# Seven block products instead of eight in the mLSTM's x and z projections of a one-core block kernel

## Chip, core and metric

One core of a Trainium2 chip runs the whole kernel. The metric is the device time of one execution in microseconds (us): the median of 3 runs is 1810.85 us, from 1810.42 to 1810.91.

## What is computed

The input is one sequence of 512 tokens with 1024 channels in f32. It goes through a first block (a gated feed-forward net, FFN; a mixer of two attentions; a second FFN) and a second block (an mLSTM mixer, then an RG-LRU mixer, with a final norm). The change touches the mLSTM:

```python
proj = u @ w_in                       # u: 512 x 1024, normed
xm, z, o_pre, i_pre, f_pre = split(proj)          # xm, z, o_pre: 512 x 2048
xc = silu(causal_dwconv(xm, conv_w, conv_b))      # 4 taps
q, k = per head: xc @ w_q, xc @ w_k               # 4 heads, 512 -> 256
v = per head: xm @ w_v                            # 512 -> 512
h_tilde = mlstm_chunkwise(q, k, v, log_i, log_f)
hh = sigmoid(o_pre) * h_tilde                     # then a norm over each head: hn
y = (hn * norm_w + skip * xc) * silu(z)
x = x + y @ w_out
```

## The kernel before, in words

Channels lie on the 128 partitions, tokens on the 512 columns. Every weight product is made of three matmuls (`mm3`, L112): each operand is split into a rounded part `hi` (fp32r) and the remainder `lo`, and hi\*hi, hi\*lo and lo\*hi add up in PSUM. A weight tile of 128 x 1024 is loaded by SyncE's queue into one of 4 `raw` tiles; ScalarE copies it to `hi` (L98), VectorE subtracts to get `lo` (L100); there are 5 tiles of each (`wload`, L93). A *group* (L148) is 24 matmuls of 512 columns: one block of 128 output channels over 8 blocks of input channels.

**The pairs of the FFN.** Both FFNs already use a seven-product scheme (Winograd's form of Strassen's) for most gate and up blocks: `Pair` (L223) and `pair_products` (L301). Two groups, 2 x 24 matmuls of 512 columns, become 7 products of 12 matmuls of 256 columns. A pair needs three split weight tiles and a half one: the top blocks (`a11`, `a12`), differences (`s1`, `s3`) from `r2`, for which GpSimd's queue issues a DMA that adds a weight from memory onto a tile (L212), two sums on VectorE (L247, L248) with their split (`s2`, `s4`), and `a22` (L251). The activations need eight combinations, made once by `xhalves` (L264), which fill 12 tiles of the pool `act` (40) and 16 of the 18 of the pool `chain`. VectorE joins the products from PSUM (L323 to L325, L335). A pair's weights are made during the pair before (`nxt`); the first pair of a run has no pair before it.

**The mLSTM** (L706 to L985) makes x, z and the output gate o by plain groups. `x_proj(hd)` and `z_proj(hd)` are four groups each, `o_proj(hd)` (L854) 96 matmuls of 512 columns. Its order is the list at L958 to L985: for heads 0 to 2 `scores`, `o_proj` (`v_proj` for head 0), `numer`, `z_proj` of the next head, `y_out`, `x_proj`, `v_proj` and `x_conv` of the next head, `out_proj`, `qk_proj`; head 3 closes. `residual` (L784) stands before `qk_proj(0)`.

**What sets the order.** Every engine has one queue and works it in order. The order in each queue is planned when the kernel is built: instructions are ranked by their place in the program, moved forward by the offset of `high_priority` (75 for weights, 100 for reads out of PSUM), and of those whose inputs and buffers the planner expects to be ready the first is taken. So matmuls of a later part may be put between those of an earlier one. DMAs of SyncE, ScalarE and GpSimd wait in that engine's queue until their buffer is free and their source is there.

Of the kernel before, what the change touches and what calls it, by code (L numbers as in the profile page):

```python
# [8 lines left out]
F32 = mybir.dt.float32  # L9
# [5 lines left out]
P = 128  # L15
# [22 lines left out]
NVEC = _n  # L38
PAD = 478


@with_exitstack
def kernel(ctx: ExitStack, tc: tile.TileContext, a, out):
# [11 lines left out]
    xp = ctx.enter_context(tc.tile_pool(name="xp", bufs=18))  # L55
    vp = ctx.enter_context(tc.tile_pool(name="vp", bufs=5))
    pp = ctx.enter_context(tc.tile_pool(name="pp", bufs=4, space=PSUM))
    qp = ctx.enter_context(tc.tile_pool(name="qp", bufs=4, space=PSUM))
# [164 lines left out]
    class Pair:  # L223


        def __init__(self, top, low):
            self.top, self.low, self.w = top, low, {}

# [22 lines left out]
        def last(self):  # L251
            with tc.high_priority(offset=BOOST):
                t = vp.tile([P, T + 32], F32, tag="v", name="v")
                nc.sync.dma_start(t[:, :T], self.low[:, T:])
                hi = vp.tile([P, T + 32], F32R, tag="v", name="v")
                S.copy(hi[:, :T], t[:, :T])
                lo = vp.tile([P, T + 32], F32R, tag="v", name="v")
                V.tensor_tensor(lo[:, :T], t[:, :T], f(hi[:, :T]), op=ALU.subtract)
            self.w["a22"] = cut((hi, lo), slice(0, T))
# [43 lines left out]
    def pair_products(pair, b, nxt, between):  # L303
# [30 lines left out]
        with tc.high_priority(offset=EVAC):  # L334
            V.tensor_tensor(t[:, HT : 3 * HT], c3, v, op=ALU.add)  # L335
        g, u = t[:, :T], t[:, T:]
        S.activation(g, g, AF.Silu)
# [3 lines left out]
    def ffn(x, gain, gu, dn, pre=None):  # L341
# [50 lines left out]
        for j in range(4, KF):  # L392
            nxt = Pair(gu[2 * j + 2], gu[2 * j + 3]) if j + 1 < KF else None
            job = down_job(j)
            job(-1)
            new.append(pair_products(cur, b, nxt, job))
            cur = nxt
            if j % 4 == 3 and j < 19:
                old, new = new, []
# [306 lines left out]
    def mlstm(x):  # L706
# [30 lines left out]
        skq = cp.tile([P, 16], F32, tag="skq", name="skq")  # L737
        V.tensor_copy(skq, vc("msk", 0, 16))
        R = slice(0, 4)
        gT, em, cT = (cp.tile([P, 16], F32, tag=n, name=n) for n in ("gT", "em", "cT"))  # L740
# [49 lines left out]

        def z_proj(hd):
            st[hd]["z2"] = [silu2(group(wload(a["mh"][hd][4 + j]), xs), rb) for j in range(4)]

        def x_proj(hd):
            xm, xr = [], []
            for j in range(4):
                ps = pre.pop(0) if pre else group(wload(a["mh"][hd][j]), xs)
                t = act_tile()
# [3 lines left out]
                xr.append(t)  # L802
            st[hd].update(xm=xm, xr=xr)

        def x_conv(hd):
            xc2, xcs = [], []
            for j, t in enumerate(st[hd].pop("xr")):
                c = conv(t, "mcw", 16, "mcb", 4 * hd + j)
# [26 lines left out]
        def qk_proj(hd):  # L835
            xcs = st[hd].pop("xcs")
            qk = []
            for i in range(2):
                w = wload(a["mh"][hd][12 + i])
                w3 = tuple(z.rearrange("p (k m) -> p k m", k=4) for z in w)  # L840
                both = gp.tile([P, 2 * T], F32R, tag="four", name="four")
                for m in range(2):
                    ps = bank()
                    for k in range(4):
                        mm3(ps, tuple(z[:, k, m * P : (m + 1) * P] for z in w3), xcs[k], k == 0, k == 3)
                    hi, lo = both[:, m * T : (m + 1) * T], act_tile(F32R)
                    scale = (1.0 / 16, 1.0)[i]
                    with tc.high_priority(offset=EVAC):
                        S.activation(hi, ps, AF.Copy, scale=scale)
                        V.scalar_tensor_tensor(lo, ps, scale, f(hi), op0=ALU.mult, op1=ALU.subtract)  # L850
                    qk.append((hi, lo))
            st[hd]["qk"] = qk

        def o_proj(hd):  # L854
# [9 lines left out]
            for b in range(4):  # L864
                t = ctile()
                with tc.high_priority(offset=EVAC):
                    S.activation(t, ops[b], AF.Tanh, scale=rsh[:, b : b + 1])
                ot.append(t)
            st[hd]["o"] = ot

        def scores(hd):
            qk = st[hd].pop("qk")
            ps = cbank()
            for b in range(4):
                c = 4 * b + hd
                PE.transpose(ps[:, b * P : (b + 1) * P], cT[:, c : c + 1].to_broadcast([P, P]), ident)
            cb = ctile()
            V.tensor_copy(cb, ps)
            sm = []
            for s in range(4):  # L880
                n = T - s * P
                ps = cbank()
                for k in range(2):
                    mm3(ps[:, :n], cut(qk[2 + k], slice(s * P, s * P + P)), cut(qk[k], slice(s * P, T)), k == 0, k == 1)
                e = ctile()
                V.tensor_scalar(e[:, :n], cb[:, s * P :], gT[:, 4 * s + hd : 4 * s + hd + 1], 0.0,
# [47 lines left out]
        def y_out(hd):  # L934
            qp, xc2, z2 = st[hd].pop("o"), st[hd].pop("xc2"), st[hd].pop("z2")
            ys = []
            for j in range(4):
# [6 lines left out]
                V.tensor_tensor(xc2[j], xc2[j], z2[j], op=ALU.mult)  # L944
                ys.append(split(xc2[j], ctile))
# [35 lines left out]
        numer(3)  # L981
# [19 lines left out]

    def conv(t, w, nt, b, i):
        c = act_tile()
        V.tensor_scalar(c, t, vc(w, 3 * nt + i), vc(b, i), op0=ALU.mult, op1=ALU.add)
        for j in range(2, -1, -1):
            s = 3 - j
            V.scalar_tensor_tensor(c[:, s:], t[:, : T - s], vc(w, j * nt + i), c[:, s:], op0=ALU.mult, op1=ALU.add)
        return c
# [297 lines left out]
```

## Time and profile before

| | |
|---|---|
| median of 3 runs | 1810.85 us |
| the profiled execution | 1810.93 us |
| its span, first to last instruction | 1809.1 us |
| TensorE (PE) busy | 1788.8 us, 99% |
| weight loads of TensorE (PEld) | 1518.8 us, 84% |
| VectorE (DVE) busy | 1244.5 us, 69% |
| ScalarE (ACT) busy | 813.7 us, 45% |
| GpSimd (POOL) busy | 66.0 us, 4% |
| mean granted clock of TensorE | 0.999 |
| DMA | 198.10 MB, mean 109 GB/s |

A matmul's row in the trace lasts longer than the distance to the next one, since matmuls overlap; their pace is read from start to start. The busy time of an engine in a stretch counts overlapping instructions once. The stretch of the mLSTM goes from 1059.5 to 1570.3 us of the span.

### The profile page before, as it was taken

Reading aid. Unit: us, or ns where it says so; the run is one execution under the profiler, and the core shown is the slowest. Engines: PE = TensorE matmul, PEld = TensorE weight load, DVE = VectorE, ACT = ScalarE, POOL = GpSimd, SP = SyncE. Lnnn points to the kernel's source line nnn. Section 1 sums busy time; section 2 is a strip of 40 time slices with the busy share of each in tenths; the row PEclk is TensorE's granted clock in tenths of the full one; section 3 lists DMA queues with packets and bytes.
Section 4 is the critical chain, followed back from the end, with each engine's and each line's share of the span. In section 5 each row is a group of like instructions: output and inputs, shape, how many; then the busy total and the mean of one; then the engine's idle time right before and its main releaser. Section 6 shows DMA issues by size and latency. Waiting matters only on the chain.

```text
span 1809.1 us, 24746 instructions
## 1 busy us (share of the span) xinstructions
PE 1788.8 (99%) x9684; PEld 1518.8 (84%) x9684; DVE 1244.5 (69%) x1992; ACT 813.7 (45%) x1207; POOL 66.0 (4%) x90
## 2 busy tenths in 40 slices
PE   8999999999999999999999999999999999999998
PEld 6899999887776688799999988888888888888887
DVE  7977777735656465887777766758366566777775
ACT  5443344524345433443444444535334444456762
POOL 1000000000000000010000000000000000000000
PEclk9999999999999999999999999999999999999999
DMA  7465555433322123265556432223222231322312
GB/s 230 113 167 155 149 153 133 140 105 97 102 82 68 50 94 105 69 171 154 153 154 155 119 108 90 71 93 94 73 92 92 67 108 59 102 91 87 99 61 73
DMA packets 74805, 198.10 MB, mean 109 GB/s; under 512 B 8000, under 2 KB 8128, under 8 KB 74688
## 3 DMA queue, kind: packets, MB, share of 16 engines
q1 hardware_dynamic: 63024, 174.35, 29.9%
q0 software_dynamic: 9792, 18.88, 6.5%
q10 hardware_dynamic: 1872, 3.29, 0.6%
q8 instruction: 76, 1.25, 0.3%
q14 instruction: 41, 0.34, 0.1%
HBM read 193.08 MB, written 2.10 MB: 108 GB/s over the span
## 4 chain that ended last, share of the span: by engine, by line
PE 92%; DVE 4%; ACT 2%; issue 1%; DMA 1%; SPq 0%; DVEq 0%; POOLq 0%; POOL 0%; ACTq 0%
PE bank L113 23%; PE bank L114 23%; PE bank L115 23%; PE cbank L113 5%; PE cbank L115 5%; PE cbank L114 5%; PE cbank L633 1%; PE cbank L601 1%; DVE chain L124 1%; PE cbank L907 1%; PE cbank L908 1%; PE cbank L909 1%; DVE act L271 1%; PE cbank L570 0%; DVE act L124 0%
## 5 line engine op out<-in xcount | busy, mean ns | idle before, releaser
L113 PE MATMUL bank<-act,hi 128*128 128x512 f32 (+1 forms) x1660 | 617.6, 373 | 8.4 <-ACT act L139 7.0
L114 PE MATMUL bank<-act,hi 128*128 128x512 f32 (+1 forms) x1660 | 615.4, 371 | 0.6 <-DVE act L140 0.5
L115 PE MATMUL bank<-act,lo 128*128 128x512 f32 (+1 forms) x1660 | 614.1, 371 | 0.7 <-DVE lo L100 0.7
L98 ACT CAST hi<-raw 128x1024 fp32r<-128x1024 f32 (+2 forms) x210 | 212.3, 1014 | 424.9 <-PE bank L114 194.8
L113 PEld LDWEIGHTS bank<-act,hi 128*128 128x128 f32 x1660 | 313.2, 189 | 66.6 <-ACT act L139 7.0
L115 PEld LDWEIGHTS bank<-act,lo 128*128 128x128 f32 x1660 | 313.5, 189 | 55.8 <-issue 1.9
L114 PEld LDWEIGHTS bank<-act,hi 128*128 128x128 f32 x1660 | 313.4, 189 | 55.3 <-DVE act L140 2.6
L100 DVE TENSOR_TENSOR lo<-raw,hi 128x1024 fp32r<-128x1024 f32 (+2 forms) x210 | 246.6, 1175 | 100.7 <-ACT hi L98 99.7
L218 ACT CAST hi<-raw 128x1024 fp32r<-128x1024 f32 x140 | 146.1, 1049 | 231.5 <-PE cbank L114 107.3
L220 DVE TENSOR_TENSOR lo<-raw,hi 128x1024 fp32r<-128x1024 f32 x140 | 170.7, 1224 | 82.4 <-ACT hi L218 78.5
L113 PE MATMUL cbank<-chain,hi 128*128 128x256 f32 x432 | 122.3, 283 | 1.7 <-ACT hi L218 1.7
L115 PE MATMUL cbank<-chain,lo 128*128 128x256 f32 x432 | 122.3, 283 | 0.9 <-DVE lo L220 0.9
L114 PE MATMUL cbank<-chain,hi 128*128 128x256 f32 x432 | 122.2, 283 | 0.0
L113 PE MATMUL cbank<-act,hi 128*128 128x256 f32 (+1 forms) x264 | 88.2, 334 | 0.0
L114 PE MATMUL cbank<-act,hi 128*128 128x256 f32 (+1 forms) x264 | 87.6, 332 | 0.0
L115 PE MATMUL cbank<-act,lo 128*128 128x256 f32 (+1 forms) x264 | 87.5, 332 | 0.0
L113 PE MATMUL bank<-hi,act 128*128 128x512 f32 x224 | 87.5, 391 | 0.0
L115 PE MATMUL bank<-hi,act 128*128 128x512 f32 x224 | 87.5, 391 | 0.0
L114 PE MATMUL bank<-lo,act 128*128 128x512 f32 x224 | 87.2, 389 | 0.0
L113 PEld LDWEIGHTS cbank<-chain,hi 128*128 128x128 f32 x432 | 82.7, 192 | 3.5 <-ACT hi L218 2.1
L115 PEld LDWEIGHTS cbank<-chain,lo 128*128 128x128 f32 x432 | 82.8, 192 | 1.4 <-DVE lo L220 1.1
L114 PEld LDWEIGHTS cbank<-chain,hi 128*128 128x128 f32 x432 | 82.8, 192 | 1.2
(292 smaller groups left out, 2575.8 us busy)
## 6 DMA issues: line engine op xcount, KB each, us to landing
raw<-in_mh_dram SPq DMA_DIRECT2D x64, 512.0 KB, 3.4
raw<-in_gu_dram SPq DMA_DIRECT2D x52, 512.0 KB, 3.6
raw<-in_gu_dram SPq DMA_DIRECT2D x72, 256.0 KB, 3.0
raw<-in_gu_dram POOLq DMA_DIRECT2D x36, 512.0 KB, 6.0
raw<-in_win_dram SPq DMA_DIRECT2D x34, 512.0 KB, 3.4
raw<-in_dn_dram SPq DMA_DIRECT2D x64, 256.0 KB, 2.9
v<-in_gu_dram SPq DMA_DIRECT2D x36, 256.0 KB, 2.7
raw<-in_mo_dram SPq DMA_DIRECT2D x16, 512.0 KB, 3.4
```

Source lines behind the costliest of these rows:

```text
L98: S.copy(hi[:, :cols], raw[:, :cols])
L100: V.tensor_tensor(lo[:, :cols], raw[:, :cols], f(hi[:, :cols]), op=ALU.subtract)
L113: PE.matmul(ps, st[0], mv[0], start=start, stop=False)
L114: PE.matmul(ps, st[0], mv[1], start=False, stop=False)
L115: PE.matmul(ps, st[1], mv[0], start=False, stop=stop)
L124: V.tensor_tensor(lo, x, f(hi), op=ALU.subtract)
L218: S.copy(hi, raw)
L220: V.tensor_tensor(lo, raw, f(hi), op=ALU.subtract)
L271: V.scalar_tensor_tensor(t, x[i], gain[:, i : i + 1], rb, op0=ALU.mult, op1=ALU.mult)
L601: PE.matmul(ps[:, :n], bq[i][ro, nb * P : nb * P + P], bk[0][ro, b0 * P : b1 * P], start=True, stop=True)
L633: PE.matmul(po[64 * g : 64 * g + 64, :], bv[0][:, kb * P + 64 * g : kb * P + 64 * g + 64], ptc, start=kb == b0, stop=kb == b1 - 1)
L907: PE.matmul(ps[:, :n], wh, vh[:, c0:c1], start=s == 0, stop=False)
```

## The change

In the mLSTM, 28 of the 32 plain groups of x and z (all but x of head 0) become 14 pairs. `xhalves` is called for the mLSTM, one `step` after each of the four `o_proj`, which all move ahead of the head loop. The gates that `o_proj` makes are stored to memory by ScalarE's queue (16 stores of 256 KB) and fetched by SyncE's queue (`o_load`, 4 loads a head) near `numer`. A run of pairs is `pair_run`; there are five: z(0, first) alone, then z(0, second), x(1), x(1); z, z, x, x for heads 1 and 2 (z of that head, x of the next); z(3), z(3). The half tile `a22` is now taken from the `raw`, `hi` and `lo` tiles (`wide`). The 16 weights of `out_proj` get their `lo` from a negated copy on ScalarE and an adding DMA of GpSimd (`adding`), with twice the offset. Several tiles move from the pool `chain` to `act`, `four` or others. The negative sign that a pair leaves on its second output goes into the scale of silu or cast and into negated taps.

```diff
-    def wload(src, cols=WU):
-        with tc.high_priority(offset=BOOST):
+    def wload(src, cols=WU, adding=False):
+        with tc.high_priority(offset=BOOST * (2 if adding else 1)):
...
             lo = wp.tile([P, WU], F32R, tag="lo", name="lo")
+            if adding:
+                S.activation(lo[:, :cols], f(hi[:, :cols]), AF.Copy, scale=-1.0)
+                G.dma_start(lo[:, :cols], src, accum_op=ALU.add)
+                return hi, lo
...
         def last(self):
...
-                t = vp.tile([P, T + 32], F32, tag="v", name="v")
+                if self.wide:
+                    t = wp.tile([P, WU], F32, tag="raw", name="raw", bufs=4)
+                    hi, lo = (wp.tile([P, WU], F32R, tag=n, name=n) for n in ("hi", "lo"))
...
-        def z_proj(hd):
-            st[hd]["z2"] = [silu2(group(wload(a["mh"][hd][4 + j]), xs), rb) for j in range(4)]
-
-        def x_proj(hd):
+        b, step = xhalves(x, g0, rb)
...
+        def pair_run(jobs):
+
+            todo = [q for q in jobs if isinstance(q, tuple)]
+            cur = pair_of(*todo.pop(0))
+            cur.load()
+            cur.first()
+            cur.sums()
+            cur.last()
+            for q in jobs:
+                if not isinstance(q, tuple):
+                    q()
+                    continue
+                n, hd, _ = q
+                nxt = pair_of(*todo.pop(0)) if todo else None
+                one, two = pair_products(cur, b, nxt, lambda i: None)
+                cur = nxt
+                for t, sign in ((one, 1), (two, -1)):
+                    if n == "z":
+                        z = act_tile()
+                        S.activation(z, t, AF.Silu, scale=float(sign))
...
+                    hi, lo = act_tile(F32R), act_tile(F32R)
+                    S.activation(hi, t, AF.Copy, scale=float(sign))
+                    if sign > 0:
+                        V.tensor_tensor(lo, t, f(hi), op=ALU.subtract)
...
@@ o_proj
-                t = ctile()
+                t = act_tile()
                 with tc.high_priority(offset=EVAC):
                     S.activation(t, ops[b], AF.Tanh, scale=rsh[:, b : b + 1])
-                ot.append(t)
+                d = dp.tile([P, T], F32, tag="og", name="og")
+                S.dma_start(d, t)
+                ot.append(d)
...
+        def o_load(hd):
+            for i in range(4):
+                t = act_tile()
+                nc.sync.dma_start(t, st[hd]["o"][i])
+                st[hd]["o"][i] = t
...
@@ out_proj
-                w = wload(a["mo"][hd][o2])
+                w = wload(a["mo"][hd][o2], adding=True)
...
-        x_proj(0)
-        z_proj(0)
+        x_first()
         gate_rows()
+        for hd in range(4):
+            o_proj(hd)
+            step(hd)
+        v_proj(0)
         x_conv(0)
-        o_proj(0)
         residual()
+        pair_run([("z", 0, 0)])
         qk_proj(0)
         for hd in range(3):
+            nx = hd + 1
             scores(hd)
-            (o_proj if hd else v_proj)(hd)
-            numer(hd)
-            z_proj(hd + 1)
+            xj = [("x", nx, 0), ("x", nx, 2)]
+            if hd == 0:
+                o_load(0)
+                pair_run([("z", 0, 2), lambda: numer(0)] + xj)
+            else:
+                pair_run([("z", hd, 0), lambda: o_load(hd), ("z", hd, 2), lambda: numer(hd)] + xj)
             y_out(hd)
-            x_proj(hd + 1)
-            v_proj(hd + 1)
-            x_conv(hd + 1)
+            v_proj(nx)
+            x_conv(nx)
             if hd < 2:
                 out_proj(hd)
             else:
-                o_proj(3)
-            qk_proj(hd + 1)
+                pair_run([("z", 3, 0), ("z", 3, 2)])
+            qk_proj(nx)
         scores(3)
+        o_load(3)
         out_proj(2, 0, 1)
```

## Rows read from the trace of the kernel before

**Rows 1.** The page's first part: busy us, share of the span, instructions of engines.

```profile
PE 1788.8 (99%) x9684; PEld 1518.8 (84%) x9684; DVE 1244.5 (69%) x1992; ACT 813.7 (45%) x1207; POOL 66.0 (4%) x90
```

**Rows 2.** Windows: the mLSTM, one head of it, four stretches of the FFNs.

```profile
core 0: us, PE busy (x) PEld busy (x) DVE busy (x) ACT busy (x) POOL busy (x), PEclk, DMA share, GB/s
1059.50:1570.30 510.80, 510.03 (x2444) 426.48 (x2444) 331.62 (x581) 227.11 (x331) 12.74 (x37) 1.00 0.27 87
1257.40:1379.90 122.50, 122.50 (x586) 102.75 (x585) 73.90 (x127) 51.24 (x74) 2.29 (x9) 1.00 0.27 86
307.10:327.20 20.10, 20.10 (x171) 20.10 (x170) 15.53 (x22) 8.80 (x14) 0.00 (x0) 1.00 0.46 133
330.00:362.00 32.00, 32.00 (x142) 26.48 (x142) 26.74 (x31) 20.78 (x24) 0.00 (x0) 1.00 0.38 125
59.00:66.00 7.00, 5.78 (x44) 5.29 (x43) 6.49 (x10) 3.85 (x6) 0.00 (x0) 1.00 0.26 80
755.00:766.00 11.00, 8.71 (x60) 7.59 (x59) 10.49 (x17) 5.55 (x8) 0.00 (x0) 1.00 0.23 69
```

**Rows 3.** Timeline of PE: start us, us, line, shape; 512 columns, then two pairs.

```profile
1040.27 0.39 PE L115 MATMUL bank<-act,lo 128*128 128x512 f32 x1
...
1059.31 0.39 PE L115 MATMUL bank<-act,lo 128*128 128x512 f32 x1
...
307.41 0.28 PE L113 MATMUL bank<-act,hi 128*128 128x256 f32 x1
...
317.48 0.28 PE L113 MATMUL bank<-act,hi 128*128 128x256 f32 x1
```

**Rows 4.** Waits of PE (us in total, times, longest): 1130 to 1148 us, then 750 to 765.

```profile
PE bank L113 <- ACT act L122: 0.5, 1, 0.5
PE cbank L113 <- ACT four L849: 0.3, 1, 0.3
...
PE cbank L115 <- DVE lo L220: 0.9, 1, 0.9
```

**Rows 5.** Groups of DVE in the first FFN, 80 to 368 us: busy, mean ns | idle.

```profile
L220 DVE TENSOR_TENSOR lo<-raw,hi 128x1024 fp32r<-128x1024 f32 x62 | 75.8, 1225 | 39.4 <-ACT hi L218 37.1 <-DMA v<-in_gu_dram 2.3
...
L324 DVE TENSOR_TENSOR act<-cbank,four 128x512 f32<-128x512 f32 x17 | 11.7, 690 | 0.6
...
L248 DVE TENSOR_TENSOR raw<-raw 128x512 f32<-128x512 f32 x16 | 10.9, 681 | 0.0
...
L325 DVE SCALAR_TENSOR_TENSOR four<-cbank,act 128x256 f32<-128x256 f32 x17 | 7.2, 424 | 0.5
```

**Rows 6.** Groups of DVE in the mLSTM, 1060 to 1571 us.

```profile
L100 DVE TENSOR_TENSOR lo<-raw,hi 128x1024 fp32r<-128x1024 f32 x83 | 101.3, 1221 | 54.0 <-ACT hi L98 53.7
...
L1007 DVE SCALAR_TENSOR_TENSOR act<-act,vec 128x511 f32<-128x511 f32 x16 | 11.9, 745 | 0.3
...
L200 DVE TENSOR_TENSOR act<-bank,rb 128x512 f32<-128x512 f32 x16 | 11.0, 690 | 34.2 <-PE bank L115 34.2
```

**Rows 7.** DMA queues (packets, MB, share of 16 engines), issues (KB, us to landing).

```profile
q1 hardware_dynamic: 63024, 174.35, 29.9%
q0 software_dynamic: 9792, 18.88, 6.5%
...
raw<-in_gu_dram POOLq DMA_DIRECT2D x36, 512.0 KB, 6.0
...
raw<-in_mo_dram SPq DMA_DIRECT2D x16, 512.0 KB, 3.4
```

**Rows 8.** Groups of POOL over the span, and of ACT in the mLSTM.

```profile
L212 POOL DMA_DIRECT2D raw<-in_gu_dram x36 | 43.7, 1213 | 700.2 <-DMA raw<-in_gu_dram 385.6 <-DVE four L338 154.8 <-DVE four L323 68.6
...
L98 ACT CAST hi<-raw 128x1024 fp32r<-128x1024 f32 x84 | 88.3, 1051 | 179.6 <-issue 79.2 <-PE bank L114 67.7 <-PE bank L115 31.8
```

**Rows 9.** Timeline of PE before `numer(0)`: `scores(0)` and `v_proj(0)` take turns.

```profile
1146.62 0.85 PE L113 MATMUL cbank<-four 128*128 128x512 f32 x4 [0.28 <-ACT four L849]
...
1147.95 0.45 PE L113 MATMUL bank<-hi,act 128*128 128x512 f32 x1
```

More of the change, by code (lines that the diff above doesn't have):

```diff
@@ L38 @@
 NVEC = _n
-PAD = 478
+PAD = 414
 @with_exitstack
@@ L223, with __init__ @@
     class Pair:
-        def __init__(self, top, low):
-            self.top, self.low, self.w = top, low, {}
+        def __init__(self, top, low, wide=False):
+            self.top, self.low, self.w, self.wide = top, low, {}, wide
         def load(self):
@@ L335, in pair_products, with hidden @@
             V.tensor_tensor(t[:, HT : 3 * HT], c3, v, op=ALU.add)
-        g, u = t[:, :T], t[:, T:]
+        return t[:, :T], t[:, T:]
+    def hidden(pair, b, nxt, between):
+        g, u = pair_products(pair, b, nxt, between)
         S.activation(g, g, AF.Silu)
@@ L395, in ffn @@
             job(-1)
-            new.append(pair_products(cur, b, nxt, job))
+            new.append(hidden(cur, b, nxt, job))
             cur = nxt
@@ L738, in mlstm @@
         V.tensor_copy(skq, vc("msk", 0, 16))
+        neg = cp.tile([P, 64], F32, tag="neg", name="neg")
+        V.tensor_scalar(neg, vc("mcw", 0, 64), -1.0, None, op0=ALU.mult)
         R = slice(0, 4)
@@ L789, in mlstm, with pair_of, x_first @@
         st = [dict() for _ in range(4)]
-        def z_proj(hd):
-            st[hd]["z2"] = [silu2(group(wload(a["mh"][hd][4 + j]), xs), rb) for j in range(4)]
-        def x_proj(hd):
+        b, step = xhalves(x, g0, rb)
+        def pair_of(n, hd, j):
+            c = j + (4 if n == "z" else 0)
+            return Pair(a["mh"][hd][c], a["mh"][hd][c + 1], True)
+        def pair_run(jobs):
[17 more added lines that the diff above has]
+                        S.activation(z, t, AF.Silu, scale=float(sign))
+                        st[hd].setdefault("z2", []).append(z)
+                        continue
+                    hi, lo = act_tile(F32R), act_tile(F32R)
+                    S.activation(hi, t, AF.Copy, scale=float(sign))
+                    if sign > 0:
+                        V.tensor_tensor(lo, t, f(hi), op=ALU.subtract)
+                    else:
+                        V.scalar_tensor_tensor(lo, t, -1.0, f(hi), op0=ALU.mult, op1=ALU.subtract)
+                    st[hd].setdefault("xm", []).append((hi, lo))
+                    st[hd].setdefault("xr", []).append((t, sign))
+        def x_first():
             xm, xr = [], []
             for j in range(4):
-                ps = pre.pop(0) if pre else group(wload(a["mh"][hd][j]), xs)
-                t = act_tile()
+                ps = pre.pop(0) if pre else group(wload(a["mh"][0][j]), xs)
+                if j % 2 == 0:
+                    four = gp.tile([P, 2 * T], F32, tag="four", name="four")
+                t = four[:, j % 2 * T : j % 2 * T + T]
                 with tc.high_priority(offset=EVAC):
@@ L801, in x_proj @@
                 xm.append(split(t))
-                xr.append(t)
-            st[hd].update(xm=xm, xr=xr)
+                xr.append((t, 1))
+            st[0].update(xm=xm, xr=xr)
         def x_conv(hd):
             xc2, xcs = [], []
-            for j, t in enumerate(st[hd].pop("xr")):
-                c = conv(t, "mcw", 16, "mcb", 4 * hd + j)
+            for j, (t, sign) in enumerate(st[hd].pop("xr")):
+                c = conv(t, "mcw", 16, "mcb", 4 * hd + j, neg if sign < 0 else None)
                 S.activation(c, c, AF.Silu)
@@ L840, in qk_proj @@
                 w3 = tuple(z.rearrange("p (k m) -> p k m", k=4) for z in w)
-                both = gp.tile([P, 2 * T], F32R, tag="four", name="four")
                 for m in range(2):
@@ L845, in qk_proj @@
                         mm3(ps, tuple(z[:, k, m * P : (m + 1) * P] for z in w3), xcs[k], k == 0, k == 3)
-                    hi, lo = both[:, m * T : (m + 1) * T], act_tile(F32R)
+                    hi, lo = act_tile(F32R), act_tile(F32R)
                     scale = (1.0 / 16, 1.0)[i]
@@ L876, in scores @@
                 PE.transpose(ps[:, b * P : (b + 1) * P], cT[:, c : c + 1].to_broadcast([P, P]), ident)
-            cb = ctile()
+            cb = vp.tile([P, T + 32], F32, tag="v", name="v")[:, :T]
             V.tensor_copy(cb, ps)
@@ L884, in scores @@
                     mm3(ps[:, :n], cut(qk[2 + k], slice(s * P, s * P + P)), cut(qk[k], slice(s * P, T)), k == 0, k == 1)
-                e = ctile()
+                e = rp.tile([P, T], F32, tag="rb", name="rb")
                 V.tensor_scalar(e[:, :n], cb[:, s * P :], gT[:, 4 * s + hd : 4 * s + hd + 1], 0.0,
@@ L944, in y_out @@
                 V.tensor_tensor(xc2[j], xc2[j], z2[j], op=ALU.mult)
[L945 removed]
+                ys.append(split(xc2[j]))
             st[hd]["y"] = ys
@@ L1000, in log1p, with conv, tap @@
         return p
-    def conv(t, w, nt, b, i):
+    def conv(t, w, nt, b, i, taps=None):
         c = act_tile()
-        V.tensor_scalar(c, t, vc(w, 3 * nt + i), vc(b, i), op0=ALU.mult, op1=ALU.add)
+        taps = vc(w, 0, 4 * nt) if taps is None else taps
+        def tap(j):
+            return taps[:, j * nt + i : j * nt + i + 1]
+        V.tensor_scalar(c, t, tap(3), vc(b, i), op0=ALU.mult, op1=ALU.add)
         for j in range(2, -1, -1):
             s = 3 - j
-            V.scalar_tensor_tensor(c[:, s:], t[:, : T - s], vc(w, j * nt + i), c[:, s:], op0=ALU.mult, op1=ALU.add)
+            V.scalar_tensor_tensor(c[:, s:], t[:, : T - s], tap(j), c[:, s:], op0=ALU.mult, op1=ALU.add)
         return c
```

5 lines of the change are left out of this document (3 added, 2 removed).

## The prediction

> **What bounds the kernel now.** I read the page's busy times first: TensorE is busy 1788.8 us, 99% of the span [rows 1], so only less work for it, or idle time of it, can move the end. The windows say the same of the stretch that is changed: in the mLSTM it is busy 510.03 of 510.80 us, VectorE 331.62, ScalarE 227.11, and DMAs fill 0.27 of their engines [rows 2]. Then the timeline of TensorE for what a matmul really costs: from start to start, 84 matmuls of 512 columns take 1059.31 - 1040.27 = 19.04 us, 0.2267 us each, and one whole seven-product pair of the FFN takes 317.48 - 307.41 = 10.07 us [rows 3], with a second one right behind it and no idle time (20.10 of 20.10 us busy) [rows 2]. Last the waits: all that TensorE waits for in the changed stretch is 0.5 + 0.3 us, on ScalarE's end of a chain, before `qk_proj(0)` and `scores(0)` [rows 4]. The granted clock is 1.00 in all these stretches, the higher of its two levels (2.4 GHz). So the mLSTM is a plain sum of matmuls, and the question is whether the other engines, which get more work, can still hide it.
>
> **The change part by part.** The sum is made against the profiled execution, 1810.9 us; the median of the runs shown is 0.08 us below it, so I use the same number for both.
>
> *Fewer matmul columns.* Two groups are 48 matmuls of 512 columns, 48 x 0.2267 = 10.88 us; a pair is 10.07 us [rows 3]. That is 0.81 us less, and 14 pairs save 11.3 us. The count of products alone would say more (one eighth of 28 groups of 5.44 us is 19.0 us), since a matmul of half the columns takes 10.07 / 84 = 0.120 us, more than half of 0.2267. The Trainium skill (TensorE: Matmul & The Clock Gate, Back-to-back issue gap) gives N / 2.4 + 2.5 ns for a warm matmul alone, 215.8 and 109.2 ns, by which an estimate of the saving would be 14 x (48 x 0.2158 - 84 x 0.1092) = 16.6 us; the rows show 227 and 120 ns, and I keep to the rows.
>
> *The eight combinations* (`xhalves`) cost VectorE, per step, some ten instructions of 256 or 512 columns at 0.42 to 0.75 us [rows 5, 6], about 5.7 us, 23 us in four steps. They lie beside four `o_proj`, 4 x 96 x 0.2267 = 87 us of matmuls that need none of them. I cost them at nothing; without that cover they would cost up to 23 us.
>
> *VectorE's load in a head.* A pair needs three `lo` of 1024 columns (3 x 1.225), two sums and one `lo` of 512 (3 x 0.68), and joins of 3 x 0.69 and 0.42: 8.2 us [rows 5]. Against it fall 16 `lo` a head (four weights each of z, x, o and out; 16 x 1.221) and 8 reads of x and z (8 x 0.690) [rows 6]; the `lo` of x itself stay. So VectorE goes from 73.9 us in a head [rows 2] to 73.9 - 19.5 - 5.5 + 4 x 8.2 = 81.7 us, while TensorE's head shrinks from 122.5 to 122.5 - 21.8 (`o_proj` moved out) - 3.2 = 97.5 us. That is 84%, up from 60%. The tail of the first FFN has the same 84% (26.74 of 32.00 us) with TensorE never idle [rows 2]. So I cost this at nothing on the average and look for places where it bunches.
>
> *First pairs.* Five runs of pairs start with no pair ahead that hides their weights. The two FFNs have such starts: TensorE loses 7.00 - 5.78 = 1.2 us and 11.00 - 8.71 = 2.3 us there, with VectorE at 93% and 95% [rows 2], one of the waits being on VectorE's `lo` [rows 4]. Here the load is lower and `scores` or `v_proj` runs ahead of the start. Bounds are 0 and 2.3 us each, 0 to 11.5 in all; I take half of the nearer one, 0.6, so 3.0 us.
>
> *Places where VectorE bunches.* Before `out_proj`, `y_out` (12 instructions of 0.69, 8.3 us) and the four `lo` of v (2.8 us) stand beside the 10.9 us of `v_proj`: 0.2 to 0.3 us too much, for heads 0 and 1, 0.6 us. Before `qk_proj(3)` more comes together: `y_out` 8.3, v 2.8, four convolutions (4 x (3 x 0.745 + 0.54), the 0.54 being an estimate from the others; 11.1), their `lo` 2.8, two z pairs 16.4, the weights of q and k 2.4, in all 43.8 us beside 32.8 us of matmuls (1.8 transposes, 10.9 and two pairs). That is 11 us short. But `out_proj(2)`, 96 matmuls or 21.8 us, is ready and in no hurry there, and the planner does put a later part between an earlier one's matmuls: `scores(0)` and `v_proj(0)` take turns [rows 9]. Bounds 0 and 11; I take the 0.8 us that the like place before `qk_proj(0)` cost [rows 4]. That place itself gets `v_proj(0)` and a pair more room, so its 0.8 us go; what comes late there next is `residual`, which only `out_proj(0)` needs.
>
> *Parking the gates.* 16 stores wait on ScalarE's queue for the tanh just before them, and 16 loads on SyncE's. 32 x 0.262 MB at 3.10 us per MB (29.9% of 1809 us for 174.35 MB [rows 7]) is 26 us of DMA time in 500 us. What waits behind a store on ScalarE are weight casts that it needs 20 us later; behind a load on SyncE, weights of the next pair. Cost nothing, bounded above by one landing of 3.4 us [rows 7] for each of four fetches, 13.6 us, if every fetch were late; I take 0 since `numer` comes a pair later or, for head 3, a 5.4 us weight later.
>
> *Adding DMAs of `out_proj`.* A weight is now load 3.4 us, cast 1.05, negated copy 1.05, GpSimd's issue 1.2, adding DMA 6.0 [rows 7, 8]: 12.7 us, where it was 3.4 + 1.05 + 1.22 = 5.7. TensorE uses one in 24 x 0.2267 = 5.44 us and five `hi`/`lo` tiles go round, so four may be on the way, 21.8 us ahead. In DMA time it is 1.6 + 3.3 us (117.6 us for 36 adding DMAs) of 5.44; a pair is 1.31 MB x 3.10 + 3.3 = 7.3 of 10.07 [rows 7]. Behind GpSimd's waiting DMAs stand the masks of `scores` and the power in `numer`, each with a pair or more before it is needed. Cost 0; the upper bound is a rival.
>
> Sum: 1810.9 - 11.3 - 0.8 + 3.0 + 0.6 + 0.8 = 1803.2 us.
>
> **The rivals.** *All hidden:* first pairs and bunches cost nothing: 1810.9 - 11.3 - 0.8 = 1798.8. For it speaks that 20 us of pairs without a plain group ran at full pace at 77% of VectorE [rows 2]; against it, both starts in the FFNs.
>
> *VectorE late before `qk_proj(3)`:* `out_proj(2)` does not fill the hole, and the 11 us stand: 1803.2 + 11 - 0.8 = 1813.4. For it: VectorE's and the pools' demand. Against it: [rows 9]. It decides from 4 us on, where the gain sinks below what can be told.
>
> *The adding DMAs hold `out_proj` (the other side):* if pairs, v, q and k keep three of the five tiles, only two weights are on the way, and each takes 12.7 / 2 = 6.35 us where TensorE needs 5.44: 0.9 us for each of 16, 14.6 us, 1817.8. It is slower than before by more than can be told from 0.7 us per weight on. Against it: the FFN's 36 adding DMAs stood behind no idle time of TensorE but at its starts. For it: there they had 15 us each, here 5.4. The Trainium skill (DMA: Bandwidth & Descriptors, SWDGE vs HWDGE vs iDMA) says that such a DMA's descriptors are written by GpSimd into memory from which VectorE's two-port modes lock it out; 1.2 us for an issue beside a VectorE at 77% shows no such delay yet.
>
> *The raw tiles run out:* with `wide` a pair takes three of four raw tiles. If the next pair's load can start only when they are free, a pair takes 3.4 + 1.2 + 6.0 + 2 x 0.68 + 1.05 + 1.22 = 14.2 us, 4.2 more than 10.07, for the nine pairs with one ahead: 1803.2 + 38 = 1841. In the two FFN pairs back to back the half tile lay elsewhere, so the rows do not exclude it.
>
> *The change saves more than said:* if a matmul of 256 columns took half of 0.2267, 14 pairs would save 19.0 us, 1795.5; the pace [rows 3] speaks against it. The formula of the Trainium skill's page named above gives a saving between the two.
>
> **How the numbers follow.** A measurement of this kernel can tell about 0.2%, 3.6 us, from no change: faster is below 1807.2, slower above 1814.5. Chances: the forecast, with its bounds up to 1807.2, 0.45; all hidden 0.16; VectorE late 0.19; adding DMAs 0.13; raw tiles 0.05; more than said 0.02. Faster is 0.45 + 0.16 + 0.02 = 0.63, same 0.19, slower 0.18. The range takes in the first three: from all hidden, 1798.0, to the end of the third case, 1814.5; 0.20 is left out.
>
> **What would show it.** Right: in the windows the mLSTM is some 8 us shorter; pairs start 10.07 us apart; VectorE in a head of about 97 us is busy some 82; the waits of TensorE add up to 3 to 6 us, at first pairs, on casts or `lo`. All hidden: no such waits. VectorE late: waits before `qk_proj(3)`, on convolutions. Adding DMAs: waits at groups that read `lo` of `out_proj`'s weights, released by GpSimd's DMA. Raw tiles: SyncE's queue waits for buffers and pairs start 14 us apart. I am wrong if pairs start over 10.3 us apart inside a run, or if TensorE's granted clock falls in a hole, which no row here shows.

## The result, and the profile after

The changed kernel takes 1834.26 us (median of 4, 1832.31 to 1835.24) against 1810.88 us for the kernel before: a ratio of 1.0125, 95% interval 1.0113 to 1.0137. It is slower by 23 us where 7.7 us less were forecast, and it lies outside the range. The profiled execution spans 1833.3 us, 24.2 more than before.

I read the changed stretch first. The windows below (columns as in [rows 2]) show the whole mLSTM of the kernel after, then six stretches of it, then three in which the granted clock had fallen.

```profile
1059.20:1594.20 535.00, 511.87 (x2952) 448.14 (x2951) 386.94 (x690) 281.36 (x409) 45.45 (x67) 0.97 0.50 135
...
1100.00:1180.00 80.00, 79.64 (x359) 65.48 (x358) 40.05 (x58) 32.46 (x46) 1.35 (x2) 1.00 0.44 139
...
1190.00:1200.00 10.00, 10.00 (x82) 9.63 (x81) 10.00 (x16) 6.10 (x9) 0.00 (x0) 1.00 0.09 17
1200.00:1222.00 22.00, 11.10 (x28) 6.78 (x27) 16.56 (x25) 12.99 (x16) 1.92 (x3) 0.63 0.37 96
1222.00:1330.00 108.00, 107.45 (x684) 97.54 (x685) 87.40 (x161) 61.88 (x95) 12.63 (x20) 1.00 0.52 134
1330.00:1460.00 130.00, 129.54 (x895) 120.45 (x894) 101.37 (x200) 72.27 (x110) 13.83 (x19) 1.00 0.55 147
...
1460.00:1530.00 70.00, 59.19 (x346) 51.34 (x346) 52.15 (x76) 40.91 (x58) 7.32 (x12) 0.93 0.63 159
...
1205.30:1222.40 17.10, 9.42 (x19) 5.89 (x20) 11.66 (x19) 12.31 (x15) 1.92 (x3) 0.51 0.31 77
1485.20:1488.60 3.40, 3.29 (x16) 3.30 (x17) 3.40 (x6) 1.50 (x4) 0.00 (x0) 0.55 0.37 145
1516.00:1522.80 6.80, 5.63 (x13) 4.12 (x14) 3.95 (x8) 5.04 (x8) 0.00 (x0) 0.52 0.50 103
```

Between 1059.20 and 1594.20 us TensorE is idle for 535.00 - 511.87 = 23 us; before it was idle for 0.8 [rows 2]. The loss is in two places, around 1200 to 1222 (half idle) and between 1460 and 1530 (10.8 us idle). The 238 us between them, two whole heads of pairs with VectorE at 78 to 81%, run with 1.0 us of idle time. And in three stretches, 27.3 us together, the granted clock is near 0.5, its lower level (1.2 GHz).

For a ledger I took every step from one matmul's start to the next in the mLSTM and set it against the pace of its shape in the kernel before (0.2267 us for 512 columns, 0.120 for 256). What is over 0.3 us counts as a wait; in the stretches at half the clock up to one more pace counts as the clock's. The waits come out above the 23 us of idle time, since a matmul's row lasts longer than its pace:

| us, mLSTM | before | after | difference |
|---|---|---|---|
| matmuls at their pace | 504.8 | 494.6 | -10.2 |
| waits | 1.1 | 26.5 | +25.4 |
| matmuls slowed by the clock | 0.0 | 8.2 | +8.2 |
| small gaps | 5.2 | 5.7 | +0.5 |

The sum is +23.9 us, the 24.2 of the span but for 0.3. Of the waits 13.1 us (and 4.1 of the clock's) lie in `qk_proj(0)`, 12.2 us (and 4.0) before and in `qk_proj(3)`. What TensorE waits for in the mLSTM after (us in total, times, longest; compare [rows 4]):

```profile
PE bank L118 <- ACT act L127: 16.0, 5, 5.5
PE bank L118 <- DVE act L878: 3.8, 1, 3.8
PE cbank L995 <- DVE four L332: 1.1, 1, 1.1
PE cbank L962 <- DVE four L332: 0.7, 2, 0.5
```

L127 is ScalarE's half of the split of a convolution's output into `hi` and `lo`, which `qk_proj` reads. L878 is VectorE's read of `v_proj` out of PSUM, which frees a bank. No wait on a weight of `out_proj` is among them. Now the first place, TensorE's timeline of the kernel after (start us, us, what, [idle before <- releaser]), five of its rows:

```profile
1201.57 0.50 PE L120 MATMUL bank<-act,lo 128*128 128x512 f32 x1
1207.13 1.22 PE L118 MATMUL bank<-act,hi 128*128 128x512 f32 x2 [5.06 <-ACT act L127]
...
1210.10 0.63 PE L118 MATMUL bank<-act,hi 128*128 128x512 f32 x1
1210.52 0.63 PE L119 MATMUL bank<-act,hi 128*128 128x512 f32 x1
...
1217.08 0.80 PE L118 MATMUL bank<-act,hi 128*128 128x512 f32 x1 [5.50 <-ACT act L127]
```

Each split comes late by itself: one matmul block, five microseconds of nothing, the next. Between two rows at 1210 the step is 0.42 us instead of 0.2267, the lower clock. The Trainium skill (TensorE: Matmul & The Clock Gate, Wait — 56ns, not 53.3ns?) gives 426.7 ns from start to start for 512 columns at the lower level; the rows agree. Why the splits are late is on VectorE's timeline:

```profile
1189.71 0.68 DVE L878 TENSOR_TENSOR act<-bank,v 128x512 fp32r<-128x512 f32 x1
1190.31 0.54 DVE L1071 TENSOR_SCALAR act<-four,vec 128x512 f32<-128x512 f32 x1
1190.77 0.75 DVE L799 SCALAR_TENSOR_TENSOR h<-h,vec,rb 128x512 f32<-128x512 f32 x1
1191.43 0.75 DVE L1074 SCALAR_TENSOR_TENSOR act<-four,vec,act 128x511 f32<-128x511 f32 x1
...
1194.73 3.40 DVE L799 SCALAR_TENSOR_TENSOR h<-h,vec,rb 128x512 f32<-128x512 f32 x5
1198.04 1.22 DVE L105 TENSOR_TENSOR lo<-raw,hi 128x1024 fp32r<-128x1024 f32 x1
1199.23 0.69 DVE L129 TENSOR_TENSOR act<-act 128x512 fp32r<-128x512 f32 x1
...
1203.89 1.22 DVE L225 TENSOR_TENSOR lo<-raw,hi 128x1024 fp32r<-128x1024 f32 x1
...
1217.06 0.69 DVE L129 TENSOR_TENSOR act<-act 128x512 fp32r<-128x512 f32 x1 [3.99 <-ACT act L127]
```

The first tap of `x_conv(0)` (L1071) starts right behind the last read of `v_proj(0)` (L878), and TensorE runs dry 11.5 us later, at 1201.8. In that time and in the holes VectorE also does `residual` (L799), weights of q, k and the next pair (L105, L225), sums and joins. It is busy 10.00 of 10 and 16.56 of 22 us in the windows above. When VectorE at last waits, at 1213, it is for ScalarE, which stands in this order:

```profile
1209.35 1.28 ACT L943 ACT_TABLE_LOAD   x1
1212.11 0.63 ACT L943 ACTIVATE rb<-rb 128x512 f32<-128x512 f32 x1 [1.48 <-DVE rb L941]
1212.76 1.28 ACT L857 ACT_TABLE_LOAD   x1
1214.05 0.63 ACT L857 ACTIVATE act<-act 128x512 f32<-128x512 f32 x1
1214.70 1.28 ACT L943 ACT_TABLE_LOAD   x1
1215.99 0.52 ACT L943 ACTIVATE rb<-rb 128x384 f32<-128x384 f32 x1
1216.42 0.60 ACT L127 CAST act<-act 128x512 fp32r<-128x512 f32 x1
```

The exponentials of `scores(0)` (L943) and the silus of the convolution (L857) take turns, each turn with 1.28 us to load a table, before the cast that `qk_proj(0)` waits for. So VectorE is late by itself at the first hole, and ScalarE's order adds to it at the second. The chain of work that ended last (start us, us, what) has the last cast and, right behind it, TensorE:

```profile
1221.26 0.63 ACT act L127
1221.93 1.31 PE bank L118 x3
```

From 1189.1 us up to that matmul this chain runs through VectorE and ScalarE alone. So the matmuls that ran at the lower clock between 1207 and 1221 cost the kernel nothing: had they been faster, TensorE would have waited that much longer for the same split. Of the 27.3 us at the lower clock the chain has TensorE in 10.1 us (0.8, 3.4 and 5.9 in the three stretches). About half of that, an estimate of 5 us, is the clock's price for the kernel; the 8.2 us of the ledger are what TensorE's matmuls lost.

At the second place the longest wait has another origin; these are a row each of ScalarE, VectorE and TensorE:

```profile
1473.15 1.05 ACT L223 CAST hi<-raw 128x1024 fp32r<-128x1024 f32 x1 [6.78 <-DMA raw<-in_mh_dram]
1474.76 0.69 DVE L834 TENSOR_TENSOR act<-four,act 128x512 fp32r<-128x512 f32 x1 [4.88 <-ACT act L832]
1485.31 0.40 PE L118 MATMUL bank<-act,hi 128*128 128x256 f32 x1 [3.76 <-DVE act L878]
```

ScalarE stands 6.78 us at a weight cast of the first z pair of head 3, until that pair's adding DMA has landed, 9.0 us after its issue. Behind the cast in ScalarE's queue stands L832, which makes the `hi` of x, so VectorE is idle for 4.88 us. From then on it is busy (9.96 of 10 us from 1475 to 1485) and reads `v_proj(3)` too late; the chain that ended last takes this way too. Two waits there are for splits of convolutions; they end at 1511.6 and 1517.2 and take 1.4 and 3.7 us.

### The profile page after: what moved, and what is told of

The parts are those of the page before. It is cut to its first block, busy times and chain, and to the rows that moved or that the text cites. A ratio compares the mean times of both kernels' runs of the same rounds, so it can differ in the third digit from the quotient of the medians.

```text
span 1833.3 us, 26217 instructions
## 1 busy us (share of the span) xinstructions
PE 1789.9 (98%) x10188; PEld 1539.8 (84%) x10188; DVE 1299.6 (71%) x2101; ACT 868.0 (47%) x1285; POOL 98.7 (5%) x120
## 3 DMA queue, kind: packets, MB, share of 16 engines
q0 software_dynamic: 15904, 34.61, 11.5%
## 4 chain that ended last, share of the span: by engine, by line
PE 84%; DVE 8%; ACT 3%; issue 2%; DMA 1%; POOL 0%; SPq 0%; DVEq 0%; POOLq 0%; ACTq 0%
PE bank L118 20%; PE bank L119 20%; PE bank L120 20%; PE cbank L118 6%; PE cbank L119 6%; PE cbank L120 6%; DMA raw<-in_mh_dram 1%; PE cbank L643 1%; PE cbank L611 1%; DVE lo L225 1%; ACT hi L223 1%; DVE act L129 1%; DVE act L1074 1%; DVE chain L129 1%; DVE act L278 1%
## 5 line engine op out<-in xcount | busy, mean ns | idle before, releaser
L99 ACT CAST hi<-raw 128x1024 fp32r<-128x1024 f32 (+2 forms) x182 | 182.6, 1006 | 318.0 <-PE bank L119 160.8
L223 ACT CAST hi<-raw 128x1024 fp32r<-128x1024 f32 x182 | 190.1, 1049 | 291.5 <-PE bank L119 112.5
L225 DVE TENSOR_TENSOR lo<-raw,hi 128x1024 fp32r<-128x1024 f32 x182 | 222.0, 1223 | 113.3 <-ACT hi L223 107.7
L105 DVE TENSOR_TENSOR lo<-raw,hi 128x1024 fp32r<-128x1024 f32 (+2 forms) x166 | 192.8, 1163 | 82.4 <-ACT hi L99 81.5
L118 PE MATMUL cbank<-chain,hi 128*128 128x256 f32 x600 | 169.8, 283 | 1.7 <-ACT hi L223 1.7
L120 PE MATMUL cbank<-chain,lo 128*128 128x256 f32 x600 | 169.8, 283 | 0.9 <-DVE lo L225 0.9
L119 PE MATMUL cbank<-chain,hi 128*128 128x256 f32 x600 | 169.7, 283 | 0.0
L118 PEld LDWEIGHTS cbank<-chain,hi 128*128 128x128 f32 x600 | 115.0, 192 | 3.5 <-ACT hi L223 2.1
L120 PEld LDWEIGHTS cbank<-chain,lo 128*128 128x128 f32 x600 | 115.0, 192 | 1.4 <-DVE lo L225 1.1
L119 PEld LDWEIGHTS cbank<-chain,hi 128*128 128x128 f32 x600 | 115.0, 192 | 1.2
L118 PE MATMUL cbank<-act,hi 128*128 128x256 f32 (+1 forms) x320 | 104.3, 326 | 0.0
L120 PE MATMUL cbank<-act,lo 128*128 128x256 f32 (+1 forms) x320 | 103.7, 324 | 0.0
L119 PE MATMUL cbank<-act,hi 128*128 128x256 f32 (+1 forms) x320 | 103.6, 324 | 0.0
```

Of the source, the lines that this page charges most:

```text
L118: PE.matmul(ps, st[0], mv[0], start=start, stop=False)
L119: PE.matmul(ps, st[0], mv[1], start=False, stop=False)
L120: PE.matmul(ps, st[1], mv[0], start=False, stop=stop)
L223: S.copy(hi, raw)
L225: V.tensor_tensor(lo, raw, f(hi), op=ALU.subtract)
```

## The experiments

My theory before the runs: VectorE's work bunches at two places whose cover of matmuls the change has shortened, and each hole costs a second time through the clock. The rivals: the adding DMAs, the parked gates, or a load that is too high everywhere.

**Is the clock a cost of its own?** `filler` puts 90 matmuls of 256 columns, which nothing reads, in front of `qk_proj(0)`; it adds 10.8 us of work and leaves nothing out.

```diff
         pair_run([("z", 0, 0)])
+        spare = bank()
+        for n in range(90):
+            PE.matmul(spare[:, L], b["t1"][n % 4][0][:, :P], b["t3"][n % 4][0], start=n == 0, stop=n == 89)
         qk_proj(0)
```

> The edit adds 90 matmuls of 256 columns, whose output nothing reads, between the pair z(0, 0) and qk_proj(0): 10.8 us of work for TensorE, in the place where it waited 12 us and where its granted clock fell to 0.5 for 17 us. Theory of the clock: the waits make room for the added work, and the clock stays at 1.0, so the 4 us that the matmuls after the waits lost at the lower clock come back: 1829 to 1832, with more work done. Theory that matmuls there were slow for another reason, or that the waits aren't waits for VectorE: 1834 to 1845.

It took 1831.41 us (ratio 1.0113, 1.0098 to 1.0128): with 10.8 us more work for TensorE it is 2.9 us faster than the changed kernel, though the two intervals overlap. The window from 1180 to 1300 us, the same as in the changed kernel and then in `filler`:

```profile
1180.00:1300.00 120.00, 108.55 (x659) 95.73 (x658) 97.59 (x173) 69.99 (x102) 12.82 (x20) 0.93 0.50 130
```

```profile
1180.00:1300.00 120.00, 116.66 (x757) 105.57 (x756) 100.06 (x175) 67.94 (x100) 12.81 (x20) 1.00 0.51 132
```

The clock stays at 1.00 there, so its fall does follow the holes. The waits fall from 13.1 to 3.7 us, so filler and waits are 14.5 us, 1.4 more than the waits alone, and the 4.1 us of slow matmuls are gone: 2.7 us gained in the profiled execution (the second place came out 2.0 us shorter too, by another order of its work). The time lies in the clock theory's range, but the run does not show the clock's price, since the planned order changed as well. In `filler` the exponentials of `scores(0)` come behind the convolutions' last cast; ScalarE's rows:

```profile
1216.86 0.62 ACT L127 CAST act<-act 128x512 fp32r<-128x512 f32 x1
1217.49 1.28 ACT L943 ACT_TABLE_LOAD   x1
```

The last cast starts 4.4 us earlier than in the changed kernel (1221.26), where the first tap had started only 0.7 us earlier, and TensorE goes on at 1217.53 instead of 1221.93. So the gain can be all of the new order: `scores(0)`'s work between the convolutions had cost some 3.7 us. No run moves the exponentials alone, but `res_out`, next but one, has them in another order too.

**What fills VectorE before `qk_proj(0)`?** `res_late` moves `residual` in the program.

```diff
-        residual()
         pair_run([("z", 0, 0)])
         qk_proj(0)
+        residual()
```

> The edit moves the eight residual instructions of VectorE (8 x 0.75 us, about 5.4 us from start to start) behind qk_proj(0). Theory of the late convolutions: the 13 us that TensorE waits before and in qk_proj(0), and 4 us of matmuls at the lower granted clock after it, come from a bunch of work on VectorE and ScalarE between v_proj(0) and qk_proj(0), of which the residual is 5.4 us; so 5 to 7 us go, about 1828. Theory of the adding DMAs: no change, 1834. Theory of general load: the waits turn up again later, within 2 us of 1834.

It took 1834.99 us (1.0132, 1.0117 to 1.0147): no gain, where 1828 was expected. The planned order still put the eight instructions between the convolutions, and the waits stayed at 13.1 us with 5.3 of the clock's: the edit did not reach the queue, so it says nothing of `residual`. `res_out` moves it a head further, out of reach.

```diff
-        residual()
...
             v_proj(nx)
+            if hd == 0:
+                residual()
             x_conv(nx)
```

> The edit puts the residual behind v_proj(1), so that VectorE does not work on it between v_proj(0) and qk_proj(0) at all (in res_late it still stood between the convolutions in VectorE's queue). Theory of the late convolutions, with VectorE's time as the limit: the 13 us of waits before qk_proj(0) shrink by the 5.4 us of the eight instructions and a part of the 4 us at the lower clock goes, so 1826 to 1829. If ScalarE's order or the buffers set the pace of the convolutions: no change, 1834.

It took 1835.22 us (1.0134, 1.0119 to 1.0149), and missed 1826 to 1829. At the first place waits and clock fell, 13.1 + 4.1 to 9.6 + 2.7 us, yet hardly by `residual`: counted from the first tap, the second cast starts only 1.0 us earlier than in the changed kernel (15.13 instead of 16.15 us), the third and the fourth 4.2. Between the second and the third the exponentials here take one turn and not two; in `filler` they come behind all the casts. And the work arrived before `qk_proj(1)` instead, where TensorE waits 3.7 us for splits up to 1311.8 and runs at the lower clock until 1318.2. VectorE has no room of 5 us at that place either. `conv_early` takes the other way: `v_proj(0)` and the convolution go ahead of the four `o_proj`, where VectorE is busy only 40.05 of 80 us (window 1100 to 1180 above), with the splits left behind.

```diff
...
         gate_rows()
+        v_proj(0)
+        x_conv(0)
         for hd in range(4):
             o_proj(hd)
             step(hd)
-        v_proj(0)
-        x_conv(0)
+        x_split(0)
...
```

> The edit moves v_proj(0) and the four convolutions of head 0 ahead of the four o_proj; only their splits stay behind. Theory of the late convolutions: the first stretch of waits goes with its lower clock, 13 + 4 us, so about 1817; the second stays. Theory of the adding DMAs: no change, 1834. Theory of general load: half of it comes back beside the pairs of head 0, about 1826.

It took 1829.78 us (1.0102, 1.0087 to 1.0117), far from 1817 and nearer to general load's 1826. The first place fell to 4.7 + 2.2 us, 10 us less, but 7.0 of them came back at the second one, which grew from 12.2 + 4.0 to 16.9 + 6.3. The new waits there, 7.7 us in `numer(3)` and 3.7 us for the weights of a z pair, needed a cause of their own (that of `numer(3)` follows below).

**What is missing before `qk_proj(3)`?** Two edits give that place matmuls as cover, and both also take the z pairs of head 3 out of it: `z3_late` puts half of `out_proj(2)` there and takes the z pairs of head 3 behind `numer(3)`; `tail` puts the whole `out_proj(2)` there, as in heads 0 and 1, and `numer(3)` between the two z pairs (and works the first four groups of `out_proj(3)` by blocks of y).

```diff
@@ z3_late
-            if hd < 2:
-                out_proj(hd)
-            else:
-                pair_run([("z", 3, 0), ("z", 3, 2)])
+            out_proj(hd, 0, 4 if hd < 2 else 2)
             qk_proj(nx)
...
         numer(3)
...
+        pair_run([("z", 3, 0), ("z", 3, 2)])
@@ tail
...
+            out_proj(hd)
             qk_proj(nx)
         scores(3)
...
+        pair_run([("z", 3, 0), lambda: o_load(3), lambda: numer(3), ("z", 3, 2)])
         y_out(3)
...
```

> The edit puts half of out_proj(2) where the two z pairs of head 3 stood, ahead of qk_proj(3), and these pairs behind numer(3). Theory of the late convolutions: the second stretch of waits (12 us, and 4 us at the lower clock) goes, up to 3 us come back where out_proj(2) stood as cover for y_out(3), so 1818 to 1822. Theory of the adding DMAs: out_proj(2) ahead of qk_proj(3) has less time for its weights, the waits stay or grow, 1834 or more.

> The edit gives head 2 the order of heads 0 and 1, which ran without waits: all of out_proj(2) before qk_proj(3), and the z pairs of head 3 around numer(3); the first four groups of out_proj(3) go by blocks of y, since nothing is left to cover y_out(3). Theory of the late convolutions: the 12 us of waits and 4 us at the lower clock of the second stretch go, and about 3 us of waiting for the first y of head 3 come, so 1819 to 1823. Theory of general load: they come back within the stretch, 1830 or more.

`z3_late` took 1828.48 us (1.0094, 1.0077 to 1.011), not 1818 to 1822: the second place fell to 8.5 + 2.9 us, one split still came 4.9 us late, and TensorE waited 1.6 us for an adding DMA of `out_proj`. `tail` took 1830.95 us (1.0112, 1.0097 to 1.0127), which by its number is general load's: no wait is left before `qk_proj(3)`, but 5.1 us of wait appeared in `numer(3)` and 3.5 us at `y_out(3)`. That the first hole is gone does not show that `out_proj(2)` covers it, since the z pair whose weights held ScalarE there is gone from it too.

**The adding DMAs.** `no_adding` makes the `lo` of `out_proj`'s weights on VectorE again.

```diff
-                w = wload(a["mo"][hd][o2], adding=True)
+                w = wload(a["mo"][hd][o2])
```

> The edit gives out_proj's 16 weights back to VectorE's subtraction; all else stays. Theory of the adding DMAs: the two stretches of waits shrink, 5 us or more faster than 1834.3. Theory of the late convolutions: the first stretch lies ahead of every out_proj and stays as it is; VectorE gets 16 x 1.22 = 19.5 us more work, of which some falls beside waits in the second stretch: 1834 to 1840.

It took 1844.27 us (1.0182, 1.0167 to 1.0197), 10 us slower than the changed kernel. That rival falls: the DMAs help. (The edit also halves the offset of these weights' priority, but TensorE waits for none of them.) Without the DMAs 4.9 us of waits on splits appear in heads 1 and 2, where the changed kernel has none:

```profile
PE bank L118 <- ACT act L127: 4.9, 4, 1.8
PE cbank L995 <- DVE four L332: 0.5, 1, 0.5
```

**All three together, and the queue.** `best` is `conv_early`, `res_out` and `tail` in one.

> conv_early, res_out and tail together. Theory of the late convolutions: both stretches of waits go but for some 2 us at the first and 3 us at the second, so 1803 to 1808, faster than the kernel before. Theory of general load: 1815 or more.

It took 1816.63 us (1813.73 to 1819.53 in 8 runs; 1.0033, 1.0022 to 1.0043), by its number again general load's. Some 14 us of waits and clock were left, 11.3 of them at the end, where VectorE waits in `numer(3)` with this row:

```profile
1518.80 0.42 DVE L969 SCALAR_TENSOR_TENSOR act<-act,cbank 128x256 f32<-128x256 f32 x1 [7.02 <-DMA act<-og]
```

It waits for a parked gate. SyncE's queue in `best` shows why the gate is late (start us, time that the row covers, what):

```profile
1490.65 20.10 SPq L97 DMA_DIRECT2D raw<-in_mo_dram  x4
1511.25 0.33 SPq L97 DMA_DIRECT2D raw<-in_rxr_dram  x1
1511.67 1.83 SPq L925 DMA_DIRECT2D act<-og  x4
```

The fetch of head 3 stands behind four weight loads of `out_proj`, which take 20.10 us because they wait for `raw` tiles to come free: one of these waits is 16.0 us, for a tile that VectorE's sum of a pair (L253) still reads. `conv_early` has the same wait (8.71 us on `og`, behind 18.90 us of such loads). `fetch_first` moves one call; `fetch_boost` gives `o_load` priority in `best` instead, and `tail_fetch` does so in `tail`.

```diff
@@ fetch_first, against best
+        o_load(3)
         scores(3)
-        pair_run([("z", 3, 0), lambda: o_load(3), lambda: numer(3), ("z", 3, 2)])
+        pair_run([("z", 3, 0), lambda: numer(3), ("z", 3, 2)])
@@ fetch_boost and tail_fetch, in o_load
-                nc.sync.dma_start(t, st[hd]["o"][i])
+                with tc.high_priority(offset=1000):
+                    nc.sync.dma_start(t, st[hd]["o"][i])
```

> best with the fetch of head 3's gates issued ahead of its scores, so that on SyncE's queue it stands in front of out_proj(3)'s weight loads, which waited 20.1 us for raw tiles with the gates behind them. If the fetch behind those loads is what numer(3) waited for, the 3.7 us wait on the gates goes, a further wait at y_out(3) of some 2 us shrinks and up to 3 us of slow matmuls with it: 1809 to 1814 us. Rival, VectorE's load alone makes the wait: the wait moves to another row and the time stays within 2 us of 1816.6.

> best with the fetches of all four heads given priority over earlier-issued loads instead of a new place for one. If the order of the queue is the cause, the same 1809 to 1814 us as with the fetch of head 3 moved by hand; if the priority only lets the planner bring in the pairs and numerators differently, within 2 us of 1816.6.

> tail (head 2 in the order of heads 0 and 1) with the fetches of the gates given priority. By the queue theory the 5.24 us wait in numer(3) goes and some of the 3.2 us of slow matmuls behind it: 1830.95 falls to 1823 to 1827, with the waits in qk_proj(0) (13.1 us and 4.1 us of slow matmuls) left as they are. By the rival, that VectorE's load alone makes the wait, it stays at 1829 to 1833.

`fetch_first` took 1805.99 us (1805.28 to 1808.36 in 8 runs; 0.9972, 0.9961 to 0.9982), faster than both kernels and than expected. (The medians of `best` and `fetch_first` are 10.6 us apart and their profiled executions 7.9, since `best`'s profiled one was its fastest.) Its SyncE queue has the gates 19.6 us earlier:

```profile
1491.67 0.33 SPq L97 DMA_DIRECT2D raw<-in_mo_dram  x1
1492.09 1.85 SPq L925 DMA_DIRECT2D act<-og  x4
1508.12 3.64 SPq L97 DMA_DIRECT2D raw<-in_mo_dram  x3
```

The end of the mLSTM, from 1460 on, keeps 2.4 us of waits and no slow matmul, where `best` had 8.3 + 3.0; the window to 1530 is full, at a clock of 1.00:

```profile
1460.00:1530.00 70.00, 69.55 (x431) 62.54 (x429) 53.18 (x109) 41.97 (x65) 9.95 (x15) 1.00 0.57 148
```

This also settles general load, which `tail` and `best` had left open. The whole mLSTM of `fetch_first`,

```profile
1059.20:1565.00 505.80, 501.16 (x2955) 443.73 (x2953) 383.00 (x690) 274.87 (x407) 45.97 (x67) 1.00 0.53 143
```

gives VectorE 383.00 us of work in 505.80, about as much as the changed kernel (386.94) in 29 us less.

The other two missed: `fetch_boost` took 1816.82 us (1.0028, 1.0017 to 1.004), `tail_fetch` 1831.02 us (1.0108, 1.0094 to 1.0122), as their kernels did without it. The priority left the queue as it was (in `fetch_boost` the loads still start at 1490.73 and the fetch at 1511.75, in `tail_fetch` at 1508.23 and 1527.34). They say nothing against the queue; only the one edit that changed its order changed the time.

## Why the prediction was wrong, point by point

**Right: what the pairs save.** 11.3 us were forecast, the ledger has 10.2. A pair of the changed kernel steps from 1250.25 to 1260.32 us, 10.07 us as in the FFN [rows 3]. So neither the rival of the raw tiles (14 us apart) nor that of a larger saving came true. The range began at 1798.0, 0.8 us below the sum of "all hidden", without a reason; nothing hangs on it.

**Wrong, the largest step: "That place itself gets `v_proj(0)` and a pair more room, so its 0.8 us go".** I looked at how many matmuls stood ahead of `qk_proj(0)`, and not at those between its inputs and it. Before, `o_proj(0)`, 21.8 us, stood behind `x_conv(0)`. The change moves all `o_proj` and `v_proj(0)` ahead of it, and only one pair, 10.07 us, stays behind; VectorE reaches the convolution after `v_proj(0)` in its own order. I wrote "what comes late there next is `residual`, which only `out_proj(0)` needs", but on an engine in order it stands in front of the convolutions as well, though taking it out (`res_out`) brought the second cast only 1.0 us forward. The sum that I made for `qk_proj(3)` would have told: with the same prices it is here, as an estimate, 32.7 us of VectorE's work (v 2.8, convolutions 11.1, their `lo` 2.8, `residual` 5.4, a pair 8.2, weights of q and k 2.4) beside 21.0 us of matmuls (10.9 and 10.07), 11.7 us short. In place of -0.8 us stand +13.1 us of waits, of which `filler` and `res_out` put some 4 down to the exponentials of `scores(0)` between the casts; that sum does not have them.

**Wrong: "I take the 0.8 us" before `qk_proj(3)`.** That `out_proj(2)` would be put into the hole was wrong: it comes after `qk_proj(3)` in the program, the planned order left it there, and its first weight's `lo` landed only at 1512.8 us. The 11 us short that I worked out look like the 12.2 us measured, but that is in part luck: 5.1 us of idle time there are waits for splits of convolutions, as the rival said, and 3.8 us come from the first z pair's weights. So the rival of VectorE late before `qk_proj(3)` came true in part, in addition to a like one that I had not seen at `qk_proj(0)`; alone it gave 1813.4 us.

**Missing: the clock.** I named a fall of the granted clock as what would prove me wrong, and gave it no price. TensorE's matmuls lost 8.2 us to it, of which an estimate of 5 us lies in the chain that ended last; `filler` shows that it follows the holes.

**Right in size by luck: first pairs.** 3.0 us were costed for five starts, spread evenly. Four cost nothing to speak of (those of heads 1 and 2 run within the 1.0 us of idle time shown above), and that of head 3 costs 3.8 us. It does so by a way that I had not seen: its weight cast waits in ScalarE's queue, and what stands behind the cast makes VectorE late.

**Right: the average load, the adding DMAs and the eight combinations.** VectorE at 78 to 81% over whole heads (84% were forecast) costs nothing. An adding DMA of an `out_proj` weight lands 8.8 us after its issue instead of 6.0 [rows 7], and in the changed kernel TensorE never waits for it; from the DMA view of the kernel after (KB, us to landing):

```profile
raw<-in_mo_dram SPq DMA_DIRECT2D x16, 512.0 KB, 4.1
lo<-in_mo_dram POOLq DMA_DIRECT2D x16, 512.0 KB, 8.8
...
act<-og SPq DMA_DIRECT2D x16, 256.0 KB, 4.8
```

The combinations are hidden behind the `o_proj` (79.64 of 80.00 us in the window 1100 to 1180).

**Half right: parking the gates.** In the changed kernel no wait of TensorE or VectorE is due to it. But I asked what stands behind a fetch and not what a fetch stands behind; once the rest of the end moved up, that became the largest wait.

What stays open: of `fetch_first`'s 5.2 us, I did not try each of its four edits without the others, and 6.0 us of waits remain in its mLSTM. Nor is it tried what the exponentials, or the first z pair of head 3, cost by themselves.

## What to carry to other kernels

When work is moved, count for each consumer the cover between its last input's start on the engine that makes it and the consumer, not all the work ahead of it; moving an independent block forward also removes it from behind something. Work out such shortages place by place even when the average load is low, and do not trust a planner to move a block across them: if the sum says 11 us short, charge 11. Do it for every engine on the way, not for the busiest alone: ScalarE, busy about half of the time, made both places worse by what stood ahead in its queue. A lower clock after a hole adds to that only where TensorE is what the rest waits for (an estimate of 5 of 8.2 us here). And in a queue that works in order, look at what a new small transfer stands behind: loads that wait for buffers hold it as long as they wait.

## What was not expected of the hardware

The granted clock fell to its lower level in or right after holes of 5.1 and 3.8 us (changed kernel), 3.4 (`best`) and 3.1 us (`conv_early`), and stayed there for 3.4 to 17.1 us, the longest time over a second hole. The length of one hole does not tell it alone: it held through one of 2.3 us in `fetch_first` and fell after one of 2.0 us in `best`, which came behind two of 0.8 and 0.7 us. And the 17.1 us cost the kernel next to nothing, since TensorE was not what the rest waited for. Handing 16 subtractions of 1.22 us from VectorE to adding DMAs that land after 8.8 us was worth 10 us (with their offset) to a kernel whose VectorE is idle over a quarter of the time.
